# Issuing the carried rows' transfers from ScalarE, and three half projections in the second attention step

## The chip, the cores and the metric

The kernel runs on one core of a Trainium2 chip. A core has a matrix engine (TensorE, PE in the profile, with its weight loads shown apart as PEld), VectorE (DVE), ScalarE (ACT), GpSimd (POOL) and SyncE (SP), which here only issues transfers between the chip's main memory and the on-chip memory, or within the latter. Each engine works through its own list of instructions in order and waits at an instruction until the semaphores it needs are set. Matmul results land in PSUM, in eight banks of 128 x 512 numbers.

The metric is the device time of one execution, in microseconds (us). Of the kernel before there are three runs: 860.56, 860.76 and 861.03, median 860.76.

## The reference, cut to what matters

One layer of a decoder on 512 tokens of width 1024, everything in float32: a mixer sublayer, a cross-attention into 256 memory tokens, a gated feed-forward layer of width 2816, and a final norm. The change lies in the mixer. One input projection gives q, k and v of eight heads of 64, the three inputs of a short convolution, and two merge gates. The attention is "stick-breaking", strictly causal, with z = q.k / 8:

```
log_fail  = where(mask, log_sigmoid(-z), 0)
log_later = cumsum(log_fail, reverse) - log_fail
weights   = where(mask, exp(log_sigmoid(z) + log_later), 0)
out       = weights @ v
```

So a key's weight needs the sum over all later keys up to the query. That sum is what is carried from one block of keys to the next.

## The kernel before, in words

**Numbers.** A float32 product is made of three reduced-precision matmuls: each operand is split into a high part (a rounding copy on ScalarE) and a low part (a subtraction on VectorE). `load_w` (lines 139 to 152) loads a 128 x 1024 weight tile on SP (L143), casts it (L150) and subtracts (L151).

**The attention stage.** Heads are taken in four pairs, and each pair's keys in four blocks of 128, from the last block to the first: 16 steps, `steps[i] = (p, kt)` with kt = 3, 2, 1, 0. In this text step i is the i-th of them, from 0. Block kt serves the queries from 128 * kt on, so the step's tiles are 128, 256, 384 and 512 wide, for each of two heads. A step consists of these parts:

- `scores` (L373): PE multiplies k by q into a PSUM tile `z` (L382, L389). ScalarE then makes the absolute value, its exponential and log(1 + it) (L396, L397, L398) and VectorE adds max(z, 0) (L399): `e`, the negated log of the failures. GpSimd masks it (L355). ScalarE copies the first row of `z` into the tile `carries[kt % 2]` (L406).
- `parts` (L408): VectorE adds the carried row of the block before to the last row of `e` (L420), and `e` is split into `l` (L369 high, ScalarE; L370 low, VectorE).
- `weights` (L428): PE multiplies a triangle of -1 by both parts of `l` into the same `z` (L433), which does the sum over keys. VectorE subtracts the first row of `z` from the copied row (L438), ScalarE takes the exponential (L441), and **a transfer moves the row from partition 0 to partition 127 of the carry tile (L444)**, where the next step's L420 reads it. Then the weights are masked (L355) and split (L449, L450).
- `values` (L454): PE multiplies the weights by v (L461).

In iteration i PE does some halves of projections, `scores(i + 1)`, `weights(i)` and `values(i - 1)`, in that order; `parts(i + 1)` follows on the other engines. PE's order is as written there (lines 518 to 538). The other engines' order is made by a scheduler that follows priorities, so it has to be read from the built program.

**The halves.** A column block of the input projection takes 24 matmuls into a PSUM tile `pr`, cut in two entries of 12: `open_project`, then a function that finishes it and reads the tile on VectorE (L294 for q and k, L315, L321 and L334 for the convolution, L307 for the gates). There are 22 blocks, 44 entries, in a fixed order: the next pair's q and k, then this pair's three convolution inputs, and gates at the end. `fill_some` (L509) does entries until their number reaches the share of the steps so far. With FILL = ((3, 2, 3, 3), (2, 2, 3, 4)) the shares add up to 44, and the steps get 3, 2, 3, 3, then 2, 2, 3, 4 three times.

```
fill_some(n_fill * sum(shares[:i + 1]) / sum(shares))
```

The tiles `pr` alternate between the two banks of the pool `pmm`. The same pool gives the tiles of the memory's mean square (L525 to L538): `var` in step 14, ahead of `scores(15)`, and `varb`, behind `values(13)`, read by ScalarE (L121) and VectorE (L124).

**SP's queue.** All loads, the copies of q (L300) and the carry transfers (L444) are issued by SP, in one order.

Of the kernel before, what the change touches and what calls it, by code (L numbers as in the profile page):

```python
# [13 lines left out]
P = 128  # L14
# [15 lines left out]
MEM_AT = (5, 7, 9, 11)  # L30
MEAN_AT = 14
EARLY = 2
FILL = ((3, 2, 3, 3), (2, 2, 3, 4))
WARM = 8
FIRST = 4

# [4 lines left out]
def hybrid_layer(ctx: ExitStack, tc: tile.TileContext, xT_d, memT_d, cols_d, wv_d, win_d,  # L41
                 wbr_d, wmix_d, wmq_d, wmk_d, wmv_d, wmo_d, wfi_d, wfo_d, out):
    nc = tc.nc
# [19 lines left out]
    def unit(s, cols=512):  # L63
        return upool.tile([P, cols], F32R, tag="u", name=nm(s), padded_shape=[P, 512])

    def tmp(s, cols=512):
        return tpool.tile([P, cols], F32, tag="t", name=nm(s), padded_shape=[P, 512])

    def f(ap):
        return ap.bitcast(F32)  # L70
# [68 lines left out]
    def load_w(src, cols=P):  # L139

        k = D // cols
        raw = wpool.tile([P, D], F32, tag="wr", name=nm("wr"))
        i = nc.sync.dma_start(raw, src)  # L143
        if count[1] < FIRST:
            count[1] += 1
            chained(i)
        hi = wpool.tile([P, k, cols], F32R, tag="wh", name=nm("wh"))
        lo = wpool.tile([P, k, cols], F32R, tag="wl", name=nm("wl"))
        h2, l2 = (t.rearrange("p k c -> p (k c)") for t in (hi, lo))
        after(nc.scalar.copy(h2, raw), lead[-1:])  # L150
        lows.append(nc.vector.tensor_tensor(out=l2, in0=raw, in1=f(h2), op=ALU.subtract))  # L151
        return hi, lo
# [191 lines left out]
    def span(kt):  # L344
        return kt * P, S - kt * P

    def by_head(t, kt):

        n = span(kt)[1]
        if 2 * n <= 512:  # L350
            return [t[0].rearrange("p (h n) -> p h n", n=n)]
        return [u[:, None, :] for u in t]

    def causal(t):
        nc.gpsimd.affine_select(out=t[:, :, :P], in_=t[:, :, :P], compare_op=ALU.is_gt, fill=0.0,  # L355
                                base=0, pattern=[[0, t.shape[1]], [1, P]], channel_multiplier=-1)
# [3 lines left out]
    carries = [lpool.tile([P, n], F32, tag=f"carry{n}", name=f"carry{n}", bufs=1)  # L360
               for n in (S, S + HS)]
# [66 lines left out]
    def weights(p, kt):  # L428
        c0, n = span(kt)
        av[p, kt] = []  # L430
        for z, both in zip(zs[p, kt], sp[p, kt]):
            for part in both:
                nc.tensor.matmul(z, negtri, part, start=False, stop=True, skip_group_check=True)  # L433
        exp_a = []
        got = first.get((p, kt), [])
        with tc.high_priority(150):
            for r, z in zip(got, zs[p, kt]):
                nc.vector.tensor_tensor(out=r, in0=r, in1=z[0:1, :], op=ALU.subtract)  # L438
            for h, z in enumerate(zs[p, kt]):
                exp_a.append(tmp("a")[:, :z.shape[1]])  # L440
                exps.append(nc.scalar.activation(exp_a[h], z, AF.Exp))  # L441
            for h, r in enumerate(got):
                w = r.shape[1]
                nc.sync.dma_start(carries[kt % 2][P - 1:P, h * w:(h + 1) * w], r)  # L444
        for a in exp_a:
            causal(by_head([a], kt)[0])
            w = a.shape[1]
            ah, al = unit("ah")[:, :w], unit("al")[:, :w]
            nc.vector.tensor_copy(ah, a)  # L449
            nc.vector.tensor_tensor(out=al, in0=a, in1=f(ah), op=ALU.subtract)  # L450
            for i in range(w // n):
                av[p, kt].append((ah[:, i * n:(i + 1) * n], al[:, i * n:(i + 1) * n]))
# [53 lines left out]
    n_fill = len(fill)  # L506
    shares = FILL[0] + (TT - 1) * FILL[1]

# [9 lines left out]
    with tc.manual_schedule(engines={mybir.EngineType.PE}):  # L518
        for i in range(len(steps) + 1):
            if i in MEM_AT:  # L520
                mem_square(MEM_AT.index(i))
            if i == MEAN_AT - 2:
                mean = squares_mean(accm[:, 0, :], MT)
            fill_some(n_fill * sum(shares[:i + 1]) / sum(shares))
            if i == MEAN_AT:  # L525
                rm = mean[0]("rm", bank=mmtile)
            if i + 1 < len(steps):
                scores(*steps[i + 1])
            if i < len(steps):
                weights(*steps[i])  # L530
            else:
                gate(EARLY, 0)
            if i + 1 < len(steps):
                parts(*steps[i + 1])
            if i > 0:
                values(*steps[i - 1])
            if i == MEAN_AT:
                rmb = mean[1]("rmb", bank=mmtile)  # L538
# [22 lines left out]
    for m in range(KD):  # L561
# [8 lines left out]
        w = load_w(wbr_d[m])  # L570
# [11 lines left out]
    for m in range(KD):  # L582
        w = load_w(wmk_d[m])
# [11 lines left out]
    for n in range(2):  # L595
        pss = [ztile("vm") for _ in range(MT)]
        for c in range(4):
            w = load_w(wmv_d[n, c], 512)
# [83 lines left out]
    for h in range(MH):  # L682
# [43 lines left out]
        for j in range(2):  # L726
# [3 lines left out]
            for m in range(MT):  # L730
                w = vm[m][c // 512]
# [204 lines left out]
    for k in range(NF - HOLD):  # L936
        w = load_w(wfo_d[k], D)
# [156 lines left out]
```

## Time and profile before

| | |
|---|---|
| median of 3 runs | 860.76 us (860.56 to 861.03) |
| the profiled execution | 860.98 us |
| its span | 859.2 us |
| attention stage, from the first projections to the last `values` | about 28 to 200 us of the span |
| PE's clock | full speed (0.999) |
| carry transfers | 16, between 50.5 and 181.4 us |

How it is read: the page's head gives each engine's busy time. A view of waits says which engine stood idle for whom. A timeline gives start, duration, engine, line, operation, result and operands of each instruction (x2: two of them merged), and in brackets the idle time just before it with what ended it. Matmuls overlap: their starts tell the pace, not their durations. "SPq" and "ACTq" are the queues of transfers issued by SP and ScalarE.

### The profile page before, as it was taken

To read this page: it belongs to the slowest core of one execution; us is meant where nothing else is said; L and a number is where in the kernel's file an instruction comes from. 1 tells how busy PE (TensorE), PEld (TensorE's weight loads), DVE (VectorE), ACT (ScalarE), POOL (GpSimd) and SP (SyncE) were. 2 spreads that over 40 slices of the span, in tenths; PEclk is the share of its full clock that TensorE was granted. 3 is DMA by queue.
4 is the path that set the end of the run, shared out by engine and by line. 5 is a ranking of instruction groups with operands and counts; after the bars stand their busy time and mean duration, and the time that the engine had idled before them with its cause. 6 is when DMAs were issued, how large, how long until landed. Compare 5 with 4: busy or idle time off the path is not lost.

```text
span 859.2 us, 12693 instructions
## 1 busy us (share of the span) xinstructions
PE 850.5 (99%) x4912; PEld 748.6 (87%) x4912; DVE 586.5 (68%) x963; ACT 431.1 (50%) x750; POOL 62.0 (7%) x92
## 2 busy tenths in 40 slices
PE   9999999999999999999999999999999999999997
PEld 7877788888888898888888889999999999888897
DVE  8769898986454475555555779888887778533334
ACT  7566766665333344433444666555445556422335
POOL 1011111111000000000000101111111100000002
PEclk9999999999999999999999999999999999999999
DMA  8322331228333255422110527776777753322202
GB/s 295 132 90 77 120 111 62 74 99 266 111 103 111 96 177 184 143 98 98 50 67 33 137 54 202 187 182 172 185 188 195 182 147 127 119 98 99 73 1 98
DMA packets 42859, 108.34 MB, mean 126 GB/s; under 512 B 4656, under 2 KB 8752, under 8 KB 42800
## 3 DMA queue, kind: packets, MB, share of 16 engines
q1 hardware_dynamic: 36528, 95.72, 32.8%
q0 software_dynamic: 5984, 11.54, 8.2%
q8 instruction: 38, 0.62, 0.3%
q10 hardware_dynamic: 288, 0.29, 0.1%
q14 instruction: 21, 0.17, 0.1%
HBM read 104.36 MB, written 2.10 MB: 124 GB/s over the span
## 4 chain that ended last, share of the span: by engine, by line
PE 96%; DVE 2%; DMA 1%; issue 0%; POOL 0%; SPq 0%; DVEq 0%; ACT 0%; POOLq 0%
PE z L801 15%; PE y L801 7%; PE pr L155 7%; PE pr L156 7%; PE pr L157 7%; PE f L156 5%; PE f L157 5%; PE f L155 5%; PE v L801 4%; PE r L156 3%; PE r L155 3%; PE r L157 3%; PE v L261 3%; PE mq L156 2%; PE mq L157 2%; PE mq L155 2%
## 5 line engine op out<-in xcount | busy, mean ns | idle before, releaser
L150 ACT CAST wh<-wr 128x1024 fp32r<-128x1024 f32 x106 | 111.1, 1050 | 222.2 <-issue 98.6
L151 DVE TENSOR_TENSOR wl<-wr,wh 128x1024 fp32r<-128x1024 f32 x106 | 129.4, 1223 | 99.4 <-ACT wh L150 99.2
L155 PE MATMUL pr<-xgh,wh 128*128 128x512 f32 x288 | 112.6, 391 | 0.0
L156 PE MATMUL pr<-xgl,wh 128*128 128x512 f32 x288 | 112.4, 390 | 0.0
L157 PE MATMUL pr<-xgh,wl 128*128 128x512 f32 x288 | 112.3, 390 | 0.0
L156 PE MATMUL f<-actl,wh 128*128 128x512 f32 (+1 forms) x208 | 74.3, 357 | 0.0
L155 PE MATMUL f<-acth,wh 128*128 128x512 f32 (+1 forms) x208 | 74.2, 357 | 0.0
L157 PE MATMUL f<-acth,wl 128*128 128x512 f32 (+1 forms) x208 | 74.1, 357 | 0.0
L801 PE MATMUL z<-xdh,wf 128*128 128x256 f32 x352 | 70.4, 283 | 0.0
L157 PEld LDWEIGHTS pr<-xgh,wl 128*128 128x128 f32 x288 | 54.1, 188 | 11.3
L155 PEld LDWEIGHTS pr<-xgh,wh 128*128 128x128 f32 x288 | 54.1, 188 | 10.9
L156 PEld LDWEIGHTS pr<-xgl,wh 128*128 128x128 f32 x288 | 54.1, 188 | 10.8
L758 POOL DMA_DIRECT2D ws<-in_w_ffn_in_dram x22 | 26.6, 1208 | 469.0 <-DVE c L616 267.8
L801 PEld LDWEIGHTS z<-xdh,wf 128*128 128x128 f32 x352 | 58.0, 192 | 0.0
L821 ACT COPY sa<-z 128x256 f32<-128x256 f32 x44 | 16.4, 372 | 78.3 <-PE z L801 78.2
L801 PE MATMUL z<-xdl,wf 128*128 128x256 f32 x176 | 49.9, 283 | 0.0
L792 DVE TENSOR_TENSOR wf<-s,wf 128x512 fp32r<-128x512 f32 x44 | 30.3, 691 | 21.1 <-ACT wf L791 20.0
L155 PEld LDWEIGHTS f<-acth,wh 128*128 128x128 f32 x208 | 39.3, 189 | 5.8
L156 PEld LDWEIGHTS f<-actl,wh 128*128 128x128 f32 x208 | 39.3, 189 | 5.6
L157 PEld LDWEIGHTS f<-acth,wl 128*128 128x128 f32 x208 | 39.3, 189 | 5.5
L801 PE MATMUL v<-xoh,wf 128*128 128x256 f32 x176 | 35.5, 283 | 0.0
L801 PE MATMUL y<-xch,wf 128*128 128x256 f32 x176 | 35.5, 283 | 0.0
(281 smaller groups left out, 2134.8 us busy)
## 6 DMA issues: line engine op xcount, KB each, us to landing
wr<-in_w_in_dram SPq DMA_DIRECT2D x36, 512.0 KB, 3.3
ws<-in_w_ffn_in_dram SPq DMA_DIRECT2D x22, 512.0 KB, 3.8
wg<-in_w_ffn_in_dram SPq DMA_DIRECT2D x22, 512.0 KB, 4.2
ws<-in_w_ffn_in_dram POOLq DMA_DIRECT2D x22, 512.0 KB, 5.8
wr<-in_w_ffn_out_dram SPq DMA_DIRECT2D x22, 512.0 KB, 3.3
a<-in_w_ffn_in_dram SPq DMA_DIRECT2D x22, 256.0 KB, 4.5
wr<-in_w_branch_dram SPq DMA_DIRECT2D x8, 512.0 KB, 3.2
wr<-in_w_mem_k_dram SPq DMA_DIRECT2D x8, 512.0 KB, 3.2
```

The costliest lines, as they stand in the source:

```text
L150: after(nc.scalar.copy(h2, raw), lead[-1:])
L151: lows.append(nc.vector.tensor_tensor(out=l2, in0=raw, in1=f(h2), op=ALU.subtract))
L155: nc.tensor.matmul(ps, a[0], b[0], start=start, stop=False, **kw)
L156: nc.tensor.matmul(ps, a[0], b[1], start=False, stop=False, **kw)
L157: nc.tensor.matmul(ps, a[1], b[0], start=False, stop=stop, **kw)
L261: nc.tensor.matmul(vps[t], xg[k][a][:, sl], wv[k][b], start=k == 0 and (a, b) == (0, 0), stop=k == KD - 1 and a == 1)
L758: nc.gpsimd.dma_start(s13, a[:, 0:4:3, :], accum_op=ALU.add)
L792: nc.vector.tensor_tensor(out=lo, in0=raw, in1=f(hi), op=ALU.subtract)
L801: nc.tensor.matmul(ps[:, :HS], a, b, start=i < 3 and k == 0 and j == 0, stop=k == KP - 1 and j == 2, skip_group_check=True)
L821: nc.scalar.copy((s[:, :HS], None, None, s[:, HS:], t[:, :HS])[i], z)
```

## The change

Two edits. The first gives step 1 a third half projection. The shares then add up to 45 for the same 44 entries, and since the number done is compared with a fraction of 44, the steps get 3, 3, 3, 3, then 2, 2, 3, 4 twice, and 2, 2, 3, 3 at the end: from step 1 to step 14 one entry more has been done at each step's end than before, and step 15 has one less. As 2 entries make a projection, what was a finished one at a step's end is now an open one, and the other way round.

The second has the carry transfer issued by ScalarE instead of SP. ScalarE's queue has otherwise one transfer at the start and one at the end.

```
-FILL = ((3, 2, 3, 3), (2, 2, 3, 4))
+FILL = ((3, 3, 3, 3), (2, 2, 3, 4))
...
             for h, r in enumerate(got):
                 w = r.shape[1]
-                nc.sync.dma_start(carries[kt % 2][P - 1:P, h * w:(h + 1) * w], r)
+                nc.scalar.dma_start(carries[kt % 2][P - 1:P, h * w:(h + 1) * w], r)
```

The built program shows two things that the diff does not. On ScalarE each carry transfer stands right behind its step's exponential L441. On VectorE and ScalarE many instructions of the stage change places with their neighbours, since the scheduler sees other times.

## The prediction

> **What bounds the kernel now.** I read the head of the page first, for the engine that is full, then what that engine waited for in the attention stage, then that stage in order of time.
>
> ```profile
> span 859.2 us, 12693 instructions
> PE 850.5 (99%) x4912; PEld 748.6 (87%) x4912; DVE 586.5 (68%) x963; ACT 431.1 (50%) x750; POOL 62.0 (7%) x92
> ```
>
> PE is busy 850.5 of 859.2 us. The change alters no matmul, so time can only come from, or go into, holes in PE's row. The waits of PE's weight loads, 28 to 215 us, are the holes of the stage that is touched:
>
> ```profile
> PEld z L433 <- DVE l L370: 2.1, 4, 0.9
> PEld z L433 <- ACT l L369: 0.4, 2, 0.2
> ```
>
> Four waits for the low part of the split `l`, 2.1 us together, and 0.4 us for the high part: about 2.5 us is all that any repair of this stage can win. In PE's timeline the two largest lie in the first pair:
>
> ```profile
> 55.79 0.49 PE L433 MATMUL z<-l,negtri 128*128 128x512 f32 x1
> 56.72 0.50 PE L433 MATMUL z<-l,negtri 128*128 128x512 f32 x1 [0.43 <-DVE l L370]
> 57.05 0.22 PE L461 MATMUL o<-ah,v 128*128 128x128 f32 x1
> ...
> 76.50 1.02 PE L433 MATMUL z<-l,negtri 128*128 128x512 f32 x3
> 77.99 0.50 PE L433 MATMUL z<-l,negtri 128*128 128x512 f32 x1 [0.47 <-DVE l L370]
> 78.33 0.33 PE L461 MATMUL o<-ah,v 128*128 128x384 f32 x1
> ...
> 92.64 0.73 PE L433 MATMUL z<-l,negtri 128*128 128x512 f32 x2
> 93.20 0.22 PE L461 MATMUL o<-ah,v 128*128 128x128 f32 x1
> ...
> 153.34 1.09 PE L433 MATMUL z<-l,negtri 128*128 128x512 f32 x4
> 154.27 0.33 PE L461 MATMUL o<-ah,v 128*128 128x384 f32 x1
> ```
>
> Step 1 takes 57.05 - 55.79 = 1.26 us for two matmuls that take 0.56 in step 5 (93.20 - 92.64): 0.70 lost. Step 3 takes 1.83 for four that take 0.93 in step 11: 0.90 lost.
>
> What was late in step 1 is the carried row, on the chain that ended last and in VectorE's waits:
>
> ```profile
> 50.50 3.79 DMA carry<-carry
> DVE e L420 <- DMA carry<-carry: 1.2, 1, 1.2
> ```
>
> It landed at 54.29; L420, L369 and L370 follow it. This is the only time that anything waited for this transfer.
>
> **The change, part by part.**
>
> *One more half projection in step 1.* A half is 12 matmuls: in step 15 one starts at 180.61 and the next at 183.35 (rows below), 2.7 us. PE reaches step 1's L433 that much later, at 58.5, while `l` is ready by about 56.7 plus at most 0.7 for one VectorE split that the changed order puts ahead of it. The wait of 0.70 goes: **-0.70**. Nothing is added to PE in all, since the shares are scaled: 44 halves over 45 shares, so each step up to 14 ends one half further on, and step 15 gets three halves instead of four.
>
> *The transfers' issue.* 16 of them go from SP to ScalarE:
>
> ```profile
> L444 SPq DMA_DIRECT2D carry<-carry x16: 502/536/580, 50.5 to 181.4; - x16
> L1024 ACTq DMA_DIRECT2D out_dram<-out x1: 350/350/350, 854.7 to 854.7; - x1
> L1024 SPq DMA_DIRECT2D out_dram<-out x3: 344/378/396, 854.1 to 855.0; - x3
> ```
>
> One form is issued on both queues, at 350 and 378 ns, so I take SP's 0.54 us for a carry on ScalarE too (bounds 0.35 and 0.58): 16 x 0.54 = 8.6 us more in ScalarE's row, which is busy 112.94 of the stage's 172 us:
>
> ```profile
> 28.00:200.00 172.00, 171.03 (x801) 139.14 (x800) 145.34 (x251) 112.94 (x210) 25.07 (x50) 1.00 0.30 100
> ```
>
> (the columns are PE, PEld, VectorE, ScalarE, GpSimd, PE's clock, DMA). SP gives up as much; it is idle between loads, and the loads keep their order, so nothing is won there. In the changed program's order the issue stands behind `exp` (L441), which already waits for the subtraction L438, so ScalarE does not wait anew for VectorE; each issue also waits for the eighth hardware transfer before it, in all 16 cases one of an earlier step (0 us). What is queued behind the issue is the next step's `exp` and `ln` (L397, L398), then L399 on VectorE, the mask on GpSimd and the carry's own consumer L420.
>
> *The landing.* SP's issues, and the transfers' view for the carries of steps 8 and 10 (KB each, us from issue to landing):
>
> ```profile
> 124.78 0.33 SPq L143 DMA_DIRECT2D wr<-in_w_in_dram  x1
> 125.21 0.54 SPq L444 DMA_DIRECT2D carry<-carry  x1
> carry<-carry SPq DMA_DIRECT2D x1, 1.0 KB, 3.3
> ...
> 140.16 0.33 SPq L143 DMA_DIRECT2D wr<-in_w_in_dram  x1
> 143.32 1.14 SPq L444 DMA_DIRECT2D carry<-carry  x2
> carry<-carry SPq DMA_DIRECT2D x2, 1.5 KB, 1.9
> ```
>
> Issued 0.43 us behind a load a carry lands after 3.3 us, 3.2 us behind one after 1.9. A queue of its own may save up to 3.3 - 1.9 = 1.4 us of landing, or nothing. It hardly matters: after step 1, L420 is held by L399 and the mask, not by the landing. I take 0. The Trainium skill's page "DMA: Bandwidth & Descriptors" (section "Issuing engines are not separate DMA queues") says that transfers from all issuing engines run on the same 16 DMA engines, and that another issuer saves only issue time. By it the landing stays at 3.3 behind a load, and the sum below would be about 0.3 us higher, in steps 3 and 5; by the rows' lower end it stands as it is. No run here shows which yet.
>
> *Step 3.* In the changed order VectorE does the convolution's five instructions ahead of L438 and a `yl` and a `wl` split (0.7 and 1.1 us) ahead of the last L370, but their input comes a half (2.7 us) earlier. Adding VectorE's and ScalarE's rows start to start from step 2 on, the last `l` is 0.4 to 1.1 us late, where it is 0.9 now; adding their full durations it is up to 1.8 late. **0**, between -0.5 and +0.9.
>
> *Step 5.* The last L370 ended 0.8 us before PE's second matmul:
>
> ```profile
> 91.14 0.68 DVE L370 TENSOR_TENSOR l<-e,l 128x512 fp32r<-128x512 f32 x1
> ```
>
> (91.82 against 92.64, and 0.23 more to the low part.) The changed order puts the weight split `wl` (1.1 us) ahead of L438, and a `qk` cast, both logs and then the 0.54 us issue around the `exp`; L370 slips by about a microsecond. **+0.2**, 0 to +0.5. Other steps keep 0.3 us or more by the same count.
>
> *Step 15, the main term.* There PE runs two matmuls into `varb` (L197) and then the remaining halves. `varb` takes one of the two banks that the projections `pr` alternate in. Until now two halves stood between `varb` and the next projection in the same bank; with the shift by one a projection is half done when step 14 ends, holding the other bank, so only **one** half stands between. That bank is free when ScalarE's L121 and VectorE's L124 have read it:
>
> ```profile
> 180.16 0.63 ACT L397 ACTIVATE e<-e 128x512 f32<-128x512 f32 x1
> 180.61 0.40 PE L155 MATMUL pr<-xgh,wh 128*128 128x512 f32 x1
> 180.84 0.49 ACT L441 ACTIVATE a<-z 128x384 f32<-128x384 f32 x1
> 181.22 0.62 ACT L398 ACTIVATE e<-e 128x512 f32<-128x512 f32 x1
> 182.06 0.68 DVE L399 SCALAR_TENSOR_TENSOR e<-z,e 128x512 f32<-128x512 f32 x1
> 182.81 0.55 POOL L355 TENSOR_SCALAR_AFFINE_SELECT e<-e 128x128 f32<-128x128 f32 x1 [0.22 <-DVE e L399]
> 183.35 0.39 PE L155 MATMUL pr<-xgh,wh 128*128 128x512 f32 x1
> 183.49 0.41 DVE L124 TENSOR_SCALAR rv<-varb 128x256 f32<-128x256 f32 x1
> 184.53 1.12 DVE L420 TENSOR_TENSOR e<-e,carry 32x384 f32<-32x384 f32 x2
> 186.07 0.39 PE L155 MATMUL pr<-xgh,wh 128*128 128x512 f32 x1
> ```
>
> Now L124 ends at 183.90 and PE wants the bank at 186.07: hidden by 2.2 us. After, PE wants it at 183.35. And L124 is later: in the changed order it stands behind the first L420. On this trace's clock: `exp` L441 180.84, the second about 0.43 later, two issues from 181.70 at 0.57 apart, L398 at 182.85 to 183.47, L399 to 184.18, the mask (0.55) to 184.80, L420 (half of 1.12) to 185.41, L124 to 185.82. PE waits 185.85 - 183.35 = 2.5 us; with issues of 0.35 and a shorter mask 1.8. The landing, at 181.70 plus 3.3 at most, is no later than 185.0 and adds 0.2 at most. I take **+2.4**, 1.8 to 2.6. `l` of step 15 is then ready before PE, which comes later.
>
> Sum: -0.70 + 0 + 0.2 + 2.4 = +1.9. The profiled execution took 860.98 us (859.2 of span and 1.8 around it); 860.98 + 1.9 = 862.9. It lies 0.22 above the median 860.76, so on the medians 862.7. Ends: -0.70 - 0.5 + 0 + 1.8 = +0.6 and -0.70 + 0.9 + 0.5 + 2.6 = +3.3, that is 861.4 to 864.1.
>
> **Rivals.** (a) *The bank wait does not bite*: L124 is reached earlier than my count, or PE finds the bank free. Then -0.70 + 0.2 and up to 0.8 of rest: 860.1 to 861.1, no change. For it: the present trace shows no such wait. Against: the changed order has L124 behind L420 and only 2.7 us of cover. (b) *Faster*: the own queue brings the rows in early enough that step 3's 0.9 goes with step 1's 0.70, with no bank wait: 860.76 - 1.6 = 859.2. It decides if landing was what held step 3; but the only recorded wait for a landing is step 1's. (c) *ScalarE becomes the bound*: each step's issues delay its weight cast L150 and split L369, and steps with little reserve (5, 9, 13, 14) stall by 0.5 to 1 us too: 2 to 4 us above the sum, 865 to 867. For it: step 13 has no reserve, its last L370 ends as PE arrives:
>
> ```profile
> 167.89 0.68 DVE L370 TENSOR_TENSOR l<-e,l 128x512 fp32r<-128x512 f32 x1
> 168.57 0.73 PE L433 MATMUL z<-l,negtri 128*128 128x512 f32 x2
> ```
>
> Against: ScalarE is a third idle, and the casts run ahead.
>
> **How the numbers follow.** The forecast has 65%, (a) 18%, (b) 5%, (c) 12%. A measurement of this kernel tells about 0.2%, 1.7 us, from no change: above 862.5 or below 859.0. The forecast's centre is just above that; I put 45 of its 65 points above it (the errors of a hand count, waits that were overlooked, mostly lengthen) and 20 within. Slower 0.45 + 0.12 = 0.57, within 0.20 + 0.18 = 0.38, faster 0.05. The range reaches down into (a) to 860.6 and up to the forecast's end and the beginning of (c), 864.4; the likeliest case alone is 861.4 to 864.1.
>
> **What would show it.** Right: PE's hole at step 1's L433 gone; one new hole of 2 to 2.5 us in step 15, at L155, released by VectorE's L124; carries on ScalarE's queue at about 0.54 us; step 3's wait about as now. Wrong: no wait of `pr` for `rv`; or new waits of L433 for L370 of over 1 us in steps 5, 9 and 13; or carries that take under 0.2 us of ScalarE, which would shorten the step 15 wait to about 1.7.

## The result, and the profile after

The changed kernel takes 863.34 us (862.79 to 864.17, eight runs), beside 860.92 us (860.56 to 861.13, eight runs) of the kernel before on the same chip: ratio 1.0029, 95% interval 1.0019 to 1.004. Its profiled execution took 863.25 us, with a span of 861.5 us where the one before had 859.2.

The busy times at the head of the changed kernel's page, then the waits of PE's weight loads and of VectorE's L420, 28 to 215 us (in total, times, longest):

```profile
PE 851.4 (99%) x4912; PEld 748.9 (87%) x4912; DVE 588.0 (68%) x963; ACT 431.4 (50%) x750; POOL 62.9 (7%) x92
```

```profile
PEld pr L155 <- DVE rv L124: 2.2, 1, 2.2
...
PEld z L433 <- DVE l L370: 2.0, 4, 1.3
```

```profile
DVE e L420 <- DMA carry<-carry: 2.2, 4, 1.4
```

PE's work is the same to 0.9 us. One wait is new, for L124, and it is nearly as large as the whole loss; the four for `l` add up to what they did before, but are not the same four. VectorE now waits four times for a carried row to land, where it waited once before. The timeline of the changed kernel, in order of time, shows steps 1, 3, 5 and 12, then step 15:

```profile
58.73 0.73 PE L433 MATMUL z<-l,negtri 128*128 128x512 f32 x2
59.29 0.22 PE L461 MATMUL o<-ah,v 128*128 128x128 f32 x1
...
78.74 0.87 PE L433 MATMUL z<-l,negtri 128*128 128x512 f32 x3
80.48 0.50 PE L433 MATMUL z<-l,negtri 128*128 128x512 f32 x1 [0.87 <-DVE l L370]
80.81 0.34 PE L461 MATMUL o<-ah,v 128*128 128x384 f32 x1
...
95.13 0.83 PE L433 MATMUL z<-l,negtri 128*128 128x512 f32 x2
95.80 0.22 PE L461 MATMUL o<-ah,v 128*128 128x128 f32 x1
...
163.74 0.59 PE L433 MATMUL z<-l,negtri 128*128 128x256 f32 x2
164.17 0.40 PE L461 MATMUL o<-ah,v 128*128 128x512 f32 x1
...
183.52 0.49 ACT L441 ACTIVATE a<-z 128x384 f32<-128x384 f32 x1
183.62 0.51 ACTq L444 DMA_DIRECT2D carry<-carry  x1
183.89 0.50 ACT L441 ACTIVATE a<-z 128x384 f32<-128x384 f32 x1
184.16 0.61 ACTq L444 DMA_DIRECT2D carry<-carry  x1
184.82 0.63 ACT L398 ACTIVATE e<-e 128x512 f32<-128x512 f32 x1 [0.43 <-ACT a L441]
185.86 0.56 DVE L450 TENSOR_TENSOR al<-a,ah 128x384 fp32r<-128x384 f32 x1
185.96 0.39 PE L157 MATMUL pr<-xgh,wl 128*128 128x512 f32 x1
186.34 0.68 DVE L399 SCALAR_TENSOR_TENSOR e<-z,e 128x512 f32<-128x512 f32 x1
187.05 0.56 DVE L420 TENSOR_TENSOR e<-e,carry 32x384 f32<-32x384 f32 x1
187.09 0.67 POOL L355 TENSOR_SCALAR_AFFINE_SELECT e<-e 128x128 f32<-128x128 f32 x1 [2.34 <-DVE e L399]
187.64 0.42 DVE L124 TENSOR_SCALAR rv<-varb 128x256 f32<-128x256 f32 x1
188.12 0.50 PE L155 MATMUL pr<-xgh,wh 128*128 128x512 f32 x1 [1.77 <-DVE rv L124]
```

Step 1's two matmuls take 59.29 - 58.73 = 0.56 us, as long as they take without a wait: the 0.70 is won. Step 3 takes 2.07 instead of 1.83: +0.24. Step 5 takes 0.67 instead of 0.56: +0.11. Step 12 takes 0.43 where it took 0.23: +0.20. In step 15 PE's next half begins 2.16 us behind the matmul at 185.96, at a pace of 0.23: +1.93. Together +1.78 of the span's 2.3. Another 0.2 lies ahead of the stage: step 0's first L433 starts at 49.17, and at 48.95 before. The other 0.3 has no row that is shown here.

The issues, by line (ns: shortest, median, longest; first and last start):

```profile
L444 ACTq DMA_DIRECT2D carry<-carry x16: 503/505/624, 50.4 to 184.2; - x16
```

### The profile page after: what moved, and what is told of

The parts are those of the page before. It is cut to its first block, busy times and chain, and to the rows that moved or that the text cites. A ratio compares the mean times of both kernels' runs of the same rounds, so it can differ in the third digit from the quotient of the medians.

```text
span 861.5 us, 12677 instructions
## 1 busy us (share of the span) xinstructions
PE 851.4 (99%) x4912; PEld 748.9 (87%) x4912; DVE 588.0 (68%) x963; ACT 431.4 (50%) x750; POOL 62.9 (7%) x92
## 4 chain that ended last, share of the span: by engine, by line
PE 95%; DVE 2%; ACT 1%; issue 0%; DMA 0%; POOL 0%; DVEq 0%; ACTq 0%; POOLq 0%
PE z L801 15%; PE y L801 7%; PE pr L155 7%; PE pr L156 7%; PE pr L157 7%; PE f L156 5%; PE f L155 5%; PE f L157 5%; PE v L801 4%; PE r L156 3%; PE r L157 3%; PE r L155 3%; PE v L261 3%; PE mq L157 2%; PE mq L156 2%; PE mq L155 2%
```

## The experiments

Theory: the fill edit brings PE back to `varb`'s bank with one half of cover instead of two, and that wait is the loss; the queue edit adds little but some length to the chain that ends in L124. Rival: the 16 issues on ScalarE are the loss, wherever the shares are. Times are compared with the kernel before on the same chip: 861.06 us for the first four runs, 861.35 for e5 to e8, 861.13 for e9 to e11, 861.38 for e12.

### Each edit alone

```
e1_fill_only:   FILL = ((3, 3, 3, 3), (2, 2, 3, 4)), L444 stays nc.sync.dma_start
e2_queue_only:  FILL = ((3, 2, 3, 3), (2, 2, 3, 4)), L444 nc.scalar.dma_start
```

> The fill edit alone; the carried rows stay on SP's queue. Theory (the bank of `varb` is wanted one half earlier because of the shares, whoever issues the rows): step 1's 0.70 us goes, and PE still waits for L124 in step 15. In this program's order L124 stands behind both L420 of step 15, one L399, one mask and one L420 more than in the changed kernel (about 0.67 + 0.55 + 0.56 = 1.8 us), while the gap of 0.4 to 0.7 us around the issues is gone and the two rows overlap in part: a wait of 1.6 to 2.4 us. Time 0.7 to 2 us above before, 861.6 to 862.9. Rival (ScalarE's issues make the loss): without them no wait of over 0.5 us in step 15, and 0.5 to 0.9 us under before, 860.0 to 860.4.

> The queue edit alone; the shares stay (3, 2, 3, 3). Theory: two halves (5.4 us) stand between `varb` and the next projection in its bank, L124 ends about 4.5 us behind `varb`, so step 15 has no wait; step 1's wait of 0.70 stays, and is 0.4 longer if the first row lands after 4.2 us again instead of 3.79; steps 3 and 12 lose 0.2 us each as in the changed kernel. Time 0 to 1 us above before, 860.9 to 861.9. Rival (ScalarE's issues make the loss wherever the shares are): 2 to 3 us above before, 863 to 864.

Measured: the fill edit alone 864.36 us, 1.0033 (1.0021 to 1.0046); the queue edit alone 863.13 us, 1.0024 (1.0016 to 1.0033). Each alone costs about as much as both together. Neither theory's range had that; with the queue edit alone the time is the rival's. The fill edit alone, PE's timeline of step 15, then a view by stretches with PE's mean granted clock (1.00 and 0.57 here) ahead of the last two columns:

```profile
185.15 0.39 PE L157 MATMUL pr<-xgh,wl 128*128 128x512 f32 x1
188.49 0.66 PE L155 MATMUL pr<-xgh,wh 128*128 128x512 f32 x1 [2.95 <-DVE rv L124]
...
192.24 0.39 PE L155 MATMUL pr<-xgh,wh 128*128 128x512 f32 x1
```

```profile
185.00:188.40 3.40, 0.54 (x3) 0.12 (x1) 3.28 (x7) 2.59 (x5) 0.90 (x2) 1.00 0.00 0
188.40:192.40 4.00, 3.91 (x10) 3.09 (x11) 3.97 (x8) 0.28 (x1) 0.00 (x0) 0.57 0.02 4
```

The bank wait is there without any issue on ScalarE, and longer: 188.49 - 185.15 - 0.23 = 3.1 us, since in this program's order L124 stands behind both L420 of the step, not one. Behind it PE runs nine matmuls in 192.24 - 188.49 = 3.75 us that take 9 x 0.227 = 2.04 at full clock: another 1.7. On the other side this kernel loses nothing in step 1 and nothing in step 3 (0.94 us for its four matmuls), 0.7 + 0.9 won. The sum, -1.6 + 3.1 + 1.7 = +3.2, is close to the +3.3 between the medians. The profiled execution is 0.8 us longer than the median of the five; its first L433 starts at 49.81, 0.86 later than before, so about as much lies ahead of the stage.

The queue edit alone, PE's rows of steps 1 and 3, then VectorE's L420 of step 9:

```profile
55.98 0.49 PE L433 MATMUL z<-l,negtri 128*128 128x512 f32 x1
57.44 0.50 PE L433 MATMUL z<-l,negtri 128*128 128x512 f32 x1 [0.97 <-DVE l L370]
...
77.23 0.41 PE L433 MATMUL z<-l,negtri 128*128 128x512 f32 x1
78.32 0.73 PE L433 MATMUL z<-l,negtri 128*128 128x512 f32 x2 [0.68 <-DVE l L370]
79.52 0.50 PE L433 MATMUL z<-l,negtri 128*128 128x512 f32 x1 [0.47 <-DVE l L370]
```

```profile
130.73 0.42 DVE L420 TENSOR_TENSOR e<-e,carry 32x256 f32<-32x256 f32 x1 [0.56 <-DMA carry<-carry]
```

No wait at the bank. But step 1 loses 1.24 us where it lost 0.70, step 3 1.70 where it lost 0.90, and steps 9 and 13 lose 0.27 and 0.33, where they lost nothing: +1.9 in the stage, and 0.2 ahead of it (the first L433 at 49.14), together the 2.1 that was measured. In step 1 the row lands no later against PE than before; the loss is in VectorE's order, where a split L170 (at 56.10) now stands ahead of L370 (56.70). In step 9 L420 waits for its row. So ScalarE's issues do cost, as the rival said; by which way is the question of e5 to e12.

### The bank wait taken away

`varb` is multiplied one step earlier, where the number of halves done is even:

```
-            if i == MEAN_AT:
+            if i == MEAN_AT - 1:
                 rmb = mean[1]("rmb", bank=mmtile)
```

e3 is the changed kernel with this, e4 the same with L444 on SP again, so the fill edit without its bank wait. e11 and e10 are the same two programs once more, beside each other on one chip.

> The changed kernel with one line more: `varb` is multiplied at the end of step 13 instead of step 14, where the count of halves done is even and two halves stand before its bank is wanted again. Theory: the wait of PE for L124 (1.93 us in the changed kernel's timeline) goes and nothing takes its place; the rest (step 1 gained, 0.2 each in steps 3, 5 and 12) stays: 863.3 - 1.9 = 861.4, between 860.9 and 862.0. Rival (the bank wait only takes up slack that PE would lose anyway behind ScalarE's later split of step 15): a wait of L433 for L370 of 1 us or more stands in step 15 instead, 862.5 to 863.5.

> The fill edit alone, with `varb` at the end of step 13 and the carried rows on SP's queue as before. Theory: step 1's 0.70 us is won, no bank wait, no issue on ScalarE: 0.3 to 0.8 us under before, 860.1 to 860.6, and about 1 us under the changed kernel with `varb` moved (the price of ScalarE's issues). Rival (the order of VectorE that the fill edit brings costs as much as it wins): within 0.3 us of before, 860.7 to 861.2.

> The fill edit with `varb` in step 13 and the rows on SP's queue, once more and beside the next run on one chip. If the gain stands: 0.7 to 1.6 us under before. If it was chance: within 0.5 us of before.

> The changed kernel with `varb` in step 13, once more on the same chip as the two others. Theory: 2.2 to 3.2 us above the run with the rows on SP's queue, as in the first comparison (862.63 against 859.94); if ScalarE's issues cost only what the second issue into an unused buffer cost (0.8 us above before), 1.6 to 2.2 us above it.

| | us | ratio to before |
|---|---|---|
| e3, rows on ScalarE's queue | 862.63 | 1.0016 (1.0007 to 1.0025) |
| e11, the same | 862.61 | 1.0017 (1.0008 to 1.0026) |
| e4, rows on SP's queue | 859.94 | 0.9986 (0.9977 to 0.9995) |
| e10, the same | 859.81 | 0.9984 (0.9975 to 0.9993) |

With the rows on SP the theory holds, and more: the fill edit without the bank wait is 1.1 and 1.3 us under the kernel before, where 0.3 to 0.8 were expected, since the wait of step 3 goes as well as that of step 1. With the rows on ScalarE the wait for L124 goes too, but the theory's 861.4 is missed: only 0.8 to 0.9 us of the 1.9 comes back, measured against before. Step 15 then loses 0.5 (e3) and 0.8 (e11) at L433, and the waits of steps 3, 5 and 12 stay. Step 15's loss isn't the queue's alone, since e10 has 0.5 of it too and e4, the same program, none: in e10 L420 waited 0.7 us there for its row. And a new wait comes at the same two banks. `var`, ahead of step 14's `scores(15)`, now takes the bank of a projection that was finished only one half earlier; in e3 and e11 VectorE reads that projection too late (L307), and step 14's L433 comes 0.6 us later behind step 13's than in e4 and e10. The waits of e11's weight loads:

```profile
PEld var L188 <- DVE g L307: 0.4, 1, 0.4
...
PEld pr L155 <- DVE g L307: 0.2, 1, 0.2
```

ScalarE's queue costs 2.7 and 2.8 us in these two pairs. By PE's rows e11 is later than e10 by 1.0 in step 3, 0.2 each in steps 5 and 12, 0.6 in step 14 and 0.3 in step 15: 2.3, the difference of the two spans (860.3 and 858.0).

How the largest part comes about is to be seen between step 2's exponentials and step 3's `l`. The timelines of ScalarE and VectorE of e10 (SP's queue), then of e11 (ScalarE's):

```profile
70.29 0.49 ACT L441 ACTIVATE a<-z 128x384 f32<-128x384 f32 x1
70.67 0.63 ACT L398 ACTIVATE e<-e 128x512 f32<-128x512 f32 x1
71.20 0.49 ACT L441 ACTIVATE a<-z 128x384 f32<-128x384 f32 x1
...
73.64 0.69 DVE L399 SCALAR_TENSOR_TENSOR e<-z,e 128x512 f32<-128x512 f32 x1
...
76.63 0.68 DVE L370 TENSOR_TENSOR l<-e,l 128x512 fp32r<-128x512 f32 x1
```

```profile
70.40 0.96 ACT L441 ACTIVATE a<-z 128x384 f32<-128x384 f32 x2
70.87 1.15 ACTq L444 DMA_DIRECT2D carry<-carry  x2
72.06 0.63 ACT L398 ACTIVATE e<-e 128x512 f32<-128x512 f32 x1 [0.71 <-ACT a L441]
...
75.60 0.68 DVE L399 SCALAR_TENSOR_TENSOR e<-z,e 128x512 f32<-128x512 f32 x1
...
79.24 0.68 DVE L370 TENSOR_TENSOR l<-e,l 128x512 fp32r<-128x512 f32 x1
```

The first log (L398) is 1.4 us later: one exponential more stands ahead of it, and two issues in a row leave ScalarE idle for 0.71. VectorE's order changes with it (a split `yl` and a split `wl` stand ahead of the last L370, and behind it in e10), the second L399 comes 2.0 later, and the last L370, which PE waits for, ends at 79.92 instead of 77.31.

### Issue, queue or order?

Three things differ between such a pair: ScalarE's time, the queue that the row travels on, and the order that the planner makes. e5 to e8 stand on e4's program (fill edit, `varb` in step 13).

```
e5: L444 on SP, and behind it nc.scalar.dma_start(spare[TT*p+kt : TT*p+kt+1, h*w:(h+1)*w], r)
e6: L444 on SP, and behind it nc.scalar.copy(spare[0:1, h*w:(h+1)*w], r)
e8: L444 on SP, and behind it nc.scalar.copy(spare[0:1, h:h+1], r[:, 0:1])
e7: L444 as nc.gpsimd.dma_start
```

> Base: the fill edit with `varb` in step 13 and the carried rows on SP's queue (859.94 us). Added: ScalarE issues a second transfer of the same row, in the place where the changed kernel issues the carried one, into a buffer that nobody reads. ScalarE's and VectorE's orders are then those of the changed kernel with `varb` in step 13 (862.63 us) but for some 10 places; only the transfer that the next step needs stays on SP. Theory (the price is ScalarE's issues and the order around them, not the queue that the row travels on): 862.1 to 863.2, with waits of L433 in steps 3, 5, 12 and 15 as there. Rival (the price is the row's later or slower transfer on the new queue): 859.6 to 860.6.

> The same base, but ScalarE makes a plain copy of the row (1x256 to 1x512, about 0.47 us as the L406 rows have it) in the place of the second issue: no second transfer, no queue. Theory (ScalarE's time in that place is the price, 0.5 us for each row whatever it is spent on): 861.7 to 863.0. Rival (an issue of a transfer holds ScalarE in a way that a plain instruction of the same length doesn't): within 0.6 us of the base, 859.5 to 860.5.

> The same base, with the carried rows issued by GpSimd: a queue of its own and no work for ScalarE, whose order stays but for some 14 places. Theory (a queue of its own is worth nothing here, ScalarE's place was the price): 859.5 to 860.6 as long as GpSimd's issue, which stands ahead of the masks L355, is not over 0.5 us; each 0.5 us more of it delays L420 and L370 by as much in the steps where the mask is on the chain, so up to 862 if it takes 1 us. Rival (any queue but SP's lands the rows late): waits of L420 for the landing of over 2 us in several steps, 862 to 864.

> The same base, with a ScalarE copy of one element of the row in place of the whole row. Theory (the price goes with the time that ScalarE spends there): shorter than the 0.47 us copy, so the price falls with it, to 860.2 to 861.8. Rival (the place alone, another instruction between the exponentials and the next step's logs, moves the orders and costs as much whatever its length): as the whole copy, 861.9 to 863.

| | us | ratio to before |
|---|---|---|
| e5, a second issue that nobody needs | 862.17 | 1.0011 (1.0002 to 1.002) |
| e6, a copy of the row on ScalarE | 862.29 | 1.0012 (1.0004 to 1.0021) |
| e8, a copy of one element | 859.65 | 0.9983 (0.9974 to 0.9992) |
| e7, rows on GpSimd's queue | 860.84 | 0.9994 (0.9985 to 1.0003) |

The row's own transfer can stay on SP and most of the price is paid (e5), and it is paid for a plain copy of the row, 0.39 to 0.60 us by its length, just as well (e6): most of the price needs no other queue, only about half a microsecond more of ScalarE in that place. Both lose 1.2 us in step 3, as e3 does. A copy of 0.18 us in the same place costs nothing (e8), less than expected. A third queue without ScalarE (e7) stands 0.6 us above e4, each against its own before, with intervals that overlap, and above the theory's 860.6. Its trace has one wait that e4 hasn't, again of a projection for its bank, ahead of step 7's `weights`:

```profile
PEld pr L155 <- DVE gb L334: 0.9, 1, 0.9
```

There the planner puts L334 behind both L370 of step 7, where e4 has it ahead of them; step 7's L433 comes 0.7 us later behind step 6's than in e4.

But e6 and e8 differ in order as well: behind the longer copy the planner puts both exponentials ahead of the first log, as in e11; behind the short one it keeps e10's order there. So e9 takes the issues out of the raised priority, which puts them behind the logs, and e12 holds the whole order:

```
e9:  the loop with L444 moved out of "with tc.high_priority(150):"
e12: e3, and at the end of the function a chain of order-only dependencies over ScalarE's and
     VectorE's instructions of the attention stage, in e4's order, with each issue behind its L441
+    for order in (ORDER_ACT, ORDER_DVE):
+        for before, behind in zip(order, order[1:]):
+            tc.add_manual_dep(by_name[f"I-{behind}"], f"I-{before}", <NoSync>, reason="order")
```

> The changed kernel with `varb` in step 13, and with ScalarE's issue taken out of the raised priority, so that in ScalarE's order it stands behind the next step's logs (L398) in nearly all steps instead of ahead of them. The count of issues, their 0.5 us each and their queue stay. Theory (the price is that the issues and the order around them delay the logs, and with them L399, L420 and L370): the logs come 0.5 to 1.2 us earlier and the price of 2.7 us falls to under half, 860.0 to 861.3. Rival (ScalarE's 8 us in all are the price, wherever they stand, or the row now lands too late for L420): waits of L433 of over 1 us stay in step 3, 862.0 to 863.2.

> The carried rows on ScalarE's queue, the fill edit and `varb` in step 13, but with ScalarE's and VectorE's instructions of the attention stage held in the order of the run with the rows on SP's queue (859.8 us, 1.3 under before); each issue is put right behind its own exponential (L441). So the 16 issues, their 0.5 us and their queue are there, and the other order that the planner makes around them isn't. Theory (the price of 2.8 us is mostly the order that the planner makes because an issue now stands on ScalarE): 0.5 to 1.3 us under before, 859.8 to 860.6, and no wait of L433 over 0.6 us. Rival (the price is the time that an issue holds ScalarE, in whatever order): 1 us or more above before, 862.0 to 863.2, with waits of L433 of about 1 us in step 3 again.

e9: 862.9 us, 1.0025 (1.0015 to 1.0035), not less than e11. The theory was right on step 3, whose wait is gone, and wrong on the sum: the planner's new order puts a `yl` split ahead of step 13's L420 and two L470 ahead of its last L370, and L420 waits 0.45 us for its row to land, which is part of what the rival said. Step 13 loses 1.2 us between its two matmuls. PE's rows there, and the stretches:

```profile
170.74 0.49 PE L433 MATMUL z<-l,negtri 128*128 128x512 f32 x1 [0.27 <-ACT l L369]
172.20 0.50 PE L433 MATMUL z<-l,negtri 128*128 128x512 f32 x1 [0.96 <-DVE l L370]
```

```profile
169.80:172.60 2.80, 1.57 (x10) 0.90 (x10) 2.68 (x5) 1.77 (x3) 0.00 (x0) 1.00 0.00 0
...
173.00:177.00 4.00, 4.00 (x13) 3.19 (x13) 3.61 (x7) 3.92 (x11) 0.90 (x3) 0.57 0.31 96
```

e12: 860.88 us, 0.9996 (0.9987 to 1.0005). The same 16 issues on the same queue as in e11, 1.7 us faster by the medians and 2.0 against the kernel before, intervals apart. It is 0.5 us under the kernel before, the lower edge of what the theory said (its times ended at 860.6). ScalarE's timeline shows why an issue is cheap there:

```profile
71.38 0.49 ACT L441 ACTIVATE a<-z 128x384 f32<-128x384 f32 x1
71.39 0.50 ACTq L444 DMA_DIRECT2D carry<-carry  x1
71.94 0.64 ACT L398 ACTIVATE e<-e 128x512 f32<-128x512 f32 x1
71.99 0.54 ACTq L444 DMA_DIRECT2D carry<-carry  x1
72.48 0.47 ACT L441 ACTIVATE a<-z 128x384 f32<-128x384 f32 x1
```

Each issue runs beside an instruction of ScalarE that is at work, and the next one starts 0.07 us behind that one's end or less. So of the 2.8 us between e10 and e11 1.7 to 2.0 is the planner's order, and 0.8 to 1.1 is left for the issues and the queue themselves; that rest is not certain, since the intervals of e12 and e10 overlap. In e12's trace 0.7 us of it is to be found: step 14 is 0.5 later than in e10, with the wait of `var` for L307 again, and steps 5 and 15 lose 0.1 each. In step 5 L420 waits 0.6 us for its row.

### The landing

From issue to landing, medians by size (1.0, 1.5, 2.0 KB):

| shares | on SP | on ScalarE |
|---|---|---|
| (3, 2, 3, 3) | 3.1, 2.7, 2.8 (before) | 4.0, 2.8, 2.7 (e2) |
| (3, 3, 3, 3) | 2.5, 1.7, 2.9 (e1) | 3.3, 1.7, 2.8 (after) |

What shortens the landing of the 1.5 KB rows is the fill edit, which moves them away from the loads: before, step 6's are issued at 105.07, right behind a load whose issue ended at 104.94; in e1 at 106.85, 3.15 us behind the load at 103.70. The queue shortens none by more than 0.1; the 1.0 KB rows land 0.8 to 0.9 later. Over all runs their medians are 2.4 to 3.1 on SP (seven runs) and 3.3 to 4.0 on ScalarE (six). Why is not shown: on SP the next load is issued behind the row (125.84 and 125.21 before), and with ScalarE's queue it goes out beside it (126.74 and 126.64 in e2). It costs little: 0.27 us in e2's step 9, 0.12 in e12's step 5. The Trainium skill's page "DMA: Bandwidth & Descriptors" (section "Issuing engines are not separate DMA queues") says that another issuer saves only issue time, since all share the same 16 DMA engines; these rows agree, and more: for the smallest rows it was slower.

## Why the prediction came out as it did

862.7 us was predicted and 863.34 measured, inside 860.6 to 864.4 and on the slower side of 0.2%. The sum of its terms, +1.9, is close to the +1.8 found in the rows; the other 0.5 of the span's 2.3 is in none of them. It is right for the mechanism that it named, and partly by luck in the sizes: step 15's is 0.5 too large, which steps 3 and 12 make up for.

- *Step 1, -0.70.* Right, as the rows show.
- *The issue, 0.54 us each.* 0.505 measured. That issues add up one behind the other on ScalarE's path was wrong in kind: an issue runs beside the activation ahead of it, so that two in a row leave a gap of 0.43 or 0.71 us where 1.14 was counted, and a single one leaves 0.2 at most.
- *Step 3, 0 (-0.5 to +0.9).* +0.24, but as the sum of two effects that the step did not have: with the fill edit alone the wait goes altogether (-0.9), and ScalarE's issues, by the order that they bring, put about 1.1 back. The prediction read only the order of the two edits together, in which they nearly cancel.
- *Step 5, +0.2.* +0.11. *Other steps keep their reserve*: step 12 did not, +0.20.
- *Step 15, +2.4 (1.8 to 2.6).* 1.93, inside the bounds and just under the 2 to 2.5 that the sign named. The place, the releaser and the one half of cover are right, a term that was mis-sized by 0.5 with errors of both signs. From the first exponential's start to the log it took 184.82 - 183.52 = 1.30 us, not 2.01. L420 did not wait for the mask: it starts 0.03 us behind L399's end, ahead of the mask's start. Against that, L399 began 0.89 us behind the log's end, because VectorE was still at the `a` splits (L450 at 185.86).
- *Landing, 0.* Right as a term; the new queue shortens none, so rival (b) had no ground. But the reason given, that after step 1 L420 is held by L399 and the mask, no longer holds in the changed kernel: L420 waits for the landing in steps 2, 5 and 6 as well as in step 1, 2.2 us in all, and step 5's 0.20 is on the way to its +0.11. The fill edit without its bank wait does come near rival (b)'s time (1.1 to 1.3 under before instead of 1.6), by another way.
- *Rival (a)*, that the bank wait does not bite, is out. *Rival (c)*, ScalarE as the bound, did not come in this kernel, but its mechanism is there: the queue edit alone stalls steps 9 and 13 by 0.3 each and costs 2.1 us.

What the prediction had wrong is how the loss divides. It charged the queue edit with about 1 us inside step 15's chain and the fill edit with the rest. In truth the fill edit alone waits longer at the bank (3.1 us, and 1.7 more at the lower clock behind it), and the queue edit alone costs 2.1. The rows show why 3.3 and 2.1 don't add up: with both edits L124 stands behind one L420 instead of two, so the pause is 1.2 us shorter and the clock stays, and the third half covers the 1.24 that the queue edit alone loses in step 1. Why the planner chooses each order was not looked into.

## What to carry to other kernels

Where an engine's order is made by a planner, an edit costs what its new order costs: read the order for each edit alone, not only for both, and when an edit's own price is wanted, hold the rest of the order fixed (e12). A tile that borrows a bank from a pool of two has a cover that depends on whether the count of uses is odd or even at that place, so a shift by one elsewhere can halve it; with the rows on SP, moving the borrower by one step made a loss of 3.3 us a gain of 1.1 to 1.3. Every borrower has to be counted anew: `var`, which stayed in its step, then cost 0.6 us where VectorE was late. A transfer issued by a busy compute engine costs little behind an instruction that it can run beside (all 16 together 0.8 to 1.1 us here, landing included), and more behind another issue.

## What was not expected of the hardware

PE's clock. Behind the 3.1 us pause of e1 the granted clock was 0.57 on average over 4 us, 1.7 us lost, while behind the 1.93 us pause of the changed kernel it stayed at 1.00. The Trainium skill's page "TensorE: Matmul & The Clock Gate" (Part 1: The HAM clock gate) says that an idle window of about 3.4 us halves the clock; e1's pause is a little shorter, and the clock fell all the same. In e9 it came behind pauses of 0.3 and 1.2 us (its rows above), in a stretch where PE still worked 1.57 of 2.80 us: by that figure it should not have. Nor does it seem to come each time: of e9's eight executions two had a mean granted clock of 0.996 and spans of 862.2 and 862.6 us, the other six 0.999 or 1.000 and 860.7 to 861.3. What decides it is open.
